# An MLP's down projection as seven block products in place of eight, woven with the up projection

## The chip, the core and the metric

The kernel runs on one core of a Trainium2 chip. The core has a matrix engine (TensorE, PE in the rows), a vector engine (VectorE, DVE), a scalar engine (ScalarE, ACT), GpSimd (POOL) and SyncE (SP), which here only issues transfers. PE reads its operands from the on-chip memory SBUF and writes sums to PSUM, which has eight banks of 128 partitions by 512 fp32 numbers. The metric is the device time of one execution in microseconds (us), lower is better.

## What is computed

One decoder layer in fp32 on 512 tokens of 2048 columns:

```
u  = rms_norm(x, norm1_w)
P  = u @ w_in                       # conv groups and gated delta heads work on P
h1 = x + concat(conv_out, delta_out) @ w_out
m  = rms_norm(h1, norm2_w) @ w_mlp_up           # 2048 x 8192
h2 = h1 + square(relu(m)) @ w_mlp_down          # 8192 x 2048
y  = rms_norm(h2, final_norm_w)
```

The change concerns the last product and what stands around it. Everything up to the output projection (`w_out`) is computed as before.

## The kernel before

**Products.** Every fp32 matrix product is made of three fp32r matmuls: each operand is split in an upper part (fp32r) and the rest, and `mm3` (lines 153 to 156 in the rows) adds upper x upper, upper x rest and rest x upper in PSUM. One matmul has a 128x128 stationary and a 128x512 moving operand. `load_pair` (L145 the load on SP, L149 ACT's cast to the upper part `whi`, L150 DVE's subtraction for the lower part `wlo`) brings a weight tile of 256 x 512 (512 KB) in a ring of three raw buffers and four pairs of split ones.

**The mixers** (conv groups and delta heads) take the first 700 us. Their buffers come from the pools `row_pool`, `inv_pool` and `tmp`, which stay open to the end of the kernel.

**Output projection.** For each of four column stretches `dc` of 512, eight weight tiles go through PE into four banks `po`, one for each 128 tokens. Then x is loaded again into `h1` and added (L739), and the squares are summed for the second norm. `norm2_columns` transposes h1 into `u2T`, 16 pairs of tiles of 128 columns by 512 tokens, without the row factors.

**The MLP** goes through 16 blocks `fb` of 512 hidden columns. `up_block(fb)` has eight steps `u`; each loads one weight tile and issues 24 matmuls into four banks `pu` (hidden columns by tokens). Then for each bank ACT takes the relu (L778), DVE multiplies it with the bank (L780), ACT and DVE split the square (L782, L783) into `hh` and `hl`, which lie in buffers of the mixers. `down_block(fb)` has eight weight tiles, two for each column stretch `dc`; each issues 24 matmuls (hidden tile stationary, weights moving) into four banks `pd`. After the second tile of a `dc` DVE adds the four banks to h1 with the squared row factor `r2`, one fp32 number for each token (L802). Since relu(r u)^2 = r^2 relu(u)^2 for r > 0, the row factors wait until there.

```
    hid = up_block(0)
    for fb in range(1, NFB):
        nxt = up_block(fb)
        down_block(fb - 1, hid)
        hid = nxt
```

So 192 matmuls of up are followed by 192 of down, 15 times; the last down product (`pl`, L833 to L842) has its 16 weight tiles split ahead of time into the buffers that `u2T` leaves, goes by tokens, and ends in the final norm (L841 to L854).

**What sets the order.** A scheduler places the instructions of each engine by the data they need and the priorities in the code (`tc.high_priority`); buffers of a pool are handed out in the order in which they come free. Weight loads are pulled ahead as far as their rings allow. PSUM: four banks in `ps_mm` (`po`, `pu`), four in `ps_aux` (`pd`, `pl`, small things).

Of the kernel before, what the change touches and what calls it, by code (L numbers as in the profile page):

```python
# [45 lines left out]
def tile_hybrid_block(ctx: ExitStack, tc: tile.TileContext, x, norm1_w, w_in, b_glu, dw_w, dw_b,  # L46
# [10 lines left out]
    row_pool = ctx.enter_context(tc.tile_pool(name="rowp", bufs=1))  # L57
# [42 lines left out]
    upper = const.tile([P, P], F32, name="upper")  # L100
# [5 lines left out]
    strict_r = const.tile([P, P], F32R, name="strict_r")  # L106
# [9 lines left out]
    sc_cols = const.tile([P, WSHORT, 3 * NH], F32, name="sc_cols")  # L116
    dw_cols = const.tile([P, WCONV, NG], F32, name="dw_cols")
# [35 lines left out]
    def mm3(ps, sta, mov, start, stop):  # L153
        nc.tensor.matmul(ps, lhsT=sta[0], rhs=mov[0], start=start, stop=False)  # L154
        nc.tensor.matmul(ps, lhsT=sta[0], rhs=mov[1], start=False, stop=False)  # L155
        nc.tensor.matmul(ps, lhsT=sta[1], rhs=mov[0], start=False, stop=stop)  # L156
# [50 lines left out]
    def transpose_half(i, groups):  # L207
        """Tokens 256 i to 256 i + 255; groups of pairs of column tiles, with their banks."""
# [110 lines left out]
    def decay_columns(pabT):  # L319
# [6 lines left out]
        ab = small.tile([P, NT, 16], F32, tag="ab", bufs=1, name="ab")  # L326
# [3 lines left out]
        def st(name, shape=(P, NT, NH)):  # L330
            return small.tile(list(shape), F32, tag=name, bufs=1, name=name)
# [28 lines left out]
        gh = small.tile([P, 2, NT, NH], F32R, tag="gh", bufs=1, name="gh")  # L360
# [72 lines left out]
    def head_keys(h, pk):  # L433
        # decay[s, c] = exp(sum of g over s < t <= c), c >= s
# [39 lines left out]
    def invert_blocks(bt, keys):  # L474
        """Transposed inverses of the 32-row diagonal blocks of I - na, by substitution."""
# [37 lines left out]
        # the transposes of y's left blocks: columns 0..63 for the blocks of 32, 64..127 for 64  # L513
# [41 lines left out]
        # upper blocks of 32, then of 64: y12 = y11 na12 y22, both blocks of a size in 64 columns  # L555
# [157 lines left out]
    for dc in range(4):  # L713
        ds = slice(dc * 512, (dc + 1) * 512)
        ps = [ps_mm.tile([P, SEQ], F32, tag="mm", name=f"po{dc}{t}") for t in range(NT)]
        for r in range(NH):
# [17 lines left out]
            if dc == 3 and 1 <= r <= 6:  # L734
                norm2_columns(range(2 * r - 2, 2 * r))
        for t in range(NT):
            h1[t][dc] = row(f"h1_{t}{dc}")
            nc.sync.dma_start(h1[t][dc], x[t * P:(t + 1) * P, ds])
            nc.vector.tensor_add(h1[t][dc], ps[t], h1[t][dc])  # L739
            square_sum(h1[t][dc], ss2[t][:, dc:dc + 1], f"j2{t}{dc}", nc.scalar)  # L740
# [14 lines left out]
    HID_TAGS = ("ug", "q", "v", "kg", "kd", "vr", "it", "y", "xx", "pc", "c0", "c1", "c2", "c3")  # L755

    def hid_pair(fb, j):
        i = (fb % 2) * 4 + j
        if i < 7:
            return (tt(HID_TAGS[2 * i], f"hh{fb}_{j}", (P, SEQ), F32R),  # L760
                    tt(HID_TAGS[2 * i + 1], f"hl{fb}_{j}", (P, SEQ), F32R))
        return tuple(row_pool.tile([P, SEQ], F32R, tag=f"row{r}", name=f"hr{fb}_{j}_{r}")
                     for r in free_rows[:2])

    def up_block(fb):
# [19 lines left out]
        return hid

    def down_block(fb, hid):
        for dc in range(4):
            ds = slice(dc * 512, (dc + 1) * 512)
            ps = [ps_aux.tile([P, SEQ], F32, tag="aux", name=f"pd{fb}_{dc}{t}") for t in range(NT)]  # L790
            for u in range(2):
                r0 = fb * FB + u * 256
                w = load_pair(w_down[r0:r0 + 256, ds].rearrange("(k p) c -> p k c", p=P),
                              [P, 2, 512], f"d{fb}_{dc}{u}")
                for t in range(NT):
                    cs = slice(t * P, (t + 1) * P)
                    for i in range(2):
                        m = hid[2 * u + i]
                        mm3(ps[t], (m[0][:, cs], m[1][:, cs]), (w[0][:, i], w[1][:, i]),
                            start=(u == 0 and i == 0), stop=(u == 1 and i == 1))  # L800
# [80 lines left out]
```

## Time and profile before

| | |
|---|---|
| three runs | 2291.12, 2291.35 and 2291.99 us, median 2291.35 |
| span of the profiled execution, first to last instruction | 2290.3 us |
| median of the runs less that span | 1.05 us |
| PE busy in the span | 2239.9 us (98%) |
| DVE, ACT, GpSimd busy | 1172.6, 691.1, 222.5 us |
| MLP | from 888.5 us to the end |

The page has the busy time of each engine over the whole span, then the span in 40 slices, the transfers, the chain of work that ended last, and groups of instructions by source line with mean durations. A matmul's row shows 389 ns, but matmuls overlap; their pace is read from how many start in a stretch. PEld is the load of a stationary operand, which goes beside PE. PEclk is the granted share of PE's full clock: 1.00 is 2.4 GHz, 0.50 is 1.2 GHz. "[4.38 <-PE pu L155]" behind a row of the timeline is the idle time of that engine before the row and the instruction that ended it.

### The profile page before, as it was taken

To read this page: it belongs to the slowest core of one execution; us is meant where nothing else is said; L and a number is where in the kernel's file an instruction comes from. 1 tells how busy PE (TensorE), PEld (TensorE's weight loads), DVE (VectorE), ACT (ScalarE), POOL (GpSimd) and SP (SyncE) were. 2 spreads that over 40 slices of the span, in tenths; PEclk is the share of its full clock that TensorE was granted. 3 is DMA by queue.
4 is the path that set the end of the run, shared out by engine and by line. 5 is a ranking of instruction groups with operands and counts; after the bars stand their busy time and mean duration, and the time that the engine had idled before them with its cause. 6 is when DMAs were issued, how large, how long until landed. Compare 5 with 4: busy or idle time off the path is not lost.

```text
span 2290.3 us, 25927 instructions
## 1 busy us (share of the span) xinstructions
PE 2239.9 (98%) x10431; PEld 1857.1 (81%) x10431; DVE 1172.6 (51%) x1671; ACT 691.1 (30%) x1153; POOL 222.5 (10%) x261
## 2 busy tenths in 40 slices
PE   6989999989999999999999999999999999999998
PEld 5877888868888888888888888888888888888886
DVE  6578677678776334344354353353353343343355
ACT  5333443324344223222122122222122222122132
POOL 3481110471110000000000000000000000000000
PEclk9999999989999999999999999999999999999999
DMA  5323223232324333333333333333333333333342
GB/s 163 106 71 83 78 79 97 79 79 77 85 83 140 100 92 92 92 101 92 101 94 100 93 101 94 99 95 98 98 96 99 95 100 93 102 92 101 92 137 84
DMA packets 189766, 220.67 MB, mean 96 GB/s; under 512 B 9901, under 2 KB 108622, under 8 KB 189646
## 3 DMA queue, kind: packets, MB, share of 16 engines
q1 hardware_dynamic: 188238, 215.34, 32.3%
q0 software_dynamic: 1408, 3.67, 0.5%
q8 instruction: 82, 1.34, 0.2%
q14 instruction: 38, 0.31, 0.0%
HBM read 212.17 MB, written 6.82 MB: 96 GB/s over the span
## 4 chain that ended last, share of the span: by engine, by line
PE 88%; POOL 6%; DVE 2%; issue 2%; DMA 2%; ACT 0%; SPq 0%; POOLq 0%; DVEq 0%; ACTq 0%
PE pu L155 10%; PE pu L154 10%; PE pu L156 10%; PE pd L154 10%; PE pd L156 10%; PE pd L155 10%; PE po L156 3%; PE po L154 3%; PE po L155 3%; POOL inv_g L496 2%; POOL inv_t L494 2%; PE pin_k L154 1%; PE pin_k L155 1%; PE pin_g L154 1%; PE pin_z L154 1%
## 5 line engine op out<-in xcount | busy, mean ns | idle before, releaser
L154 PE MATMUL pu<-v_h,whi_u 128*128 128x512 f32 x1024 | 398.4, 389 | 0.0
L155 PE MATMUL pu<-v_l,whi_u 128*128 128x512 f32 x1024 | 398.3, 389 | 0.0
L156 PE MATMUL pu<-v_h,wlo_u 128*128 128x512 f32 x1024 | 398.3, 389 | 0.0
L150 DVE TENSOR_TENSOR wlo_u<-wraw_u,whi_u 128x1024 fp32r<-128x1024 f32 x128 | 156.8, 1225 | 413.6 <-ACT whi_u L149 413.6
L154 PE MATMUL pd<-whi_d,hh 128*128 128x512 f32 x848 | 329.9, 389 | 0.0
L155 PE MATMUL pd<-wlo_d,hh 128*128 128x512 f32 x848 | 329.9, 389 | 0.0
L156 PE MATMUL pd<-whi_d,hl 128*128 128x512 f32 x848 | 329.9, 389 | 0.0
L149 ACT CAST whi_u<-wraw_u 128x1024 fp32r<-128x1024 f32 x128 | 135.0, 1055 | 543.2 <-PE pu L155 285.8
L150 DVE TENSOR_TENSOR wlo_d<-wraw_d,whi_d 128x1024 fp32r<-128x1024 f32 x120 | 147.0, 1225 | 295.6 <-ACT whi_d L149 295.6
L149 ACT CAST whi_d<-wraw_d 128x1024 fp32r<-128x1024 f32 x120 | 126.6, 1055 | 417.0 <-PE pd L156 216.0
L154 PEld LDWEIGHTS pu<-v_h,whi_u 128*128 128x128 f32 x1024 | 192.2, 188 | 39.9
L156 PEld LDWEIGHTS pu<-v_h,wlo_u 128*128 128x128 f32 x1024 | 192.2, 188 | 39.9
L155 PEld LDWEIGHTS pu<-v_l,whi_u 128*128 128x128 f32 x1024 | 192.2, 188 | 39.8
L802 DVE SCALAR_TENSOR_TENSOR h<-pd,r,h 128x512 f32<-128x512 f32 x240 | 174.4, 747 | 62.4 <-PE pd L156 62.4
L381 DVE SCALAR_TENSOR_TENSOR cacc<-chh,dw_cols,cacc 128x511 f32<-128x511 f32 (+14 forms) x240 | 195.5, 815 | 8.4 <-ACT cacc L378 5.1
L154 PEld LDWEIGHTS pd<-whi_d,hh 128*128 128x128 f32 x848 | 159.2, 188 | 33.1
L155 PEld LDWEIGHTS pd<-wlo_d,hh 128*128 128x128 f32 x848 | 159.2, 188 | 33.0
L156 PEld LDWEIGHTS pd<-whi_d,hl 128*128 128x128 f32 x848 | 159.2, 188 | 33.1
L167 POOL TENSOR_TENSOR rs_rf<-rs_sf,neg_half 128x1 f32<-128x1 f32 x4 | 2.2, 546 | 1549.0 <-DVE rs_sf L165 1549.0
L154 PE MATMUL po<-whi_o,m_h 128*128 128x512 f32 x256 | 101.0, 394 | 0.0
L156 PE MATMUL po<-whi_o,m_l 128*128 128x512 f32 x256 | 100.2, 391 | 0.0
L155 PE MATMUL po<-wlo_o,m_h 128*128 128x512 f32 x256 | 99.9, 390 | 0.0
(291 smaller groups left out, 3400.1 us busy)
## 6 DMA issues: line engine op xcount, KB each, us to landing
wraw_u<-in_w_mlp_up SPq DMA_DIRECT2D x128, 512.0 KB, 3.7
wraw_d<-in_w_mlp_down SPq DMA_DIRECT2D x120, 512.0 KB, 3.6
wraw_o<-in_w_out SPq DMA_DIRECT2D x32, 512.0 KB, 4.2
wraw_k<-in_w_in SPq DMA_DIRECT2D x16, 512.0 KB, 4.1
wraw_a<-in_w_in SPq DMA_DIRECT2D x16, 512.0 KB, 3.7
wraw_g<-in_w_in SPq DMA_DIRECT2D x16, 512.0 KB, 3.8
wraw_q<-in_w_in SPq DMA_DIRECT2D x16, 512.0 KB, 3.7
wraw_v<-in_w_in SPq DMA_DIRECT2D x16, 512.0 KB, 3.8
```

Source lines behind the costliest of these rows:

```text
L149: nc.scalar.copy(hi, raw)
L150: sub.tensor_sub(lo, raw, hi.bitcast(F32))
L154: nc.tensor.matmul(ps, lhsT=sta[0], rhs=mov[0], start=start, stop=False)
L155: nc.tensor.matmul(ps, lhsT=sta[0], rhs=mov[1], start=False, stop=False)
L156: nc.tensor.matmul(ps, lhsT=sta[1], rhs=mov[0], start=False, stop=stop)
L167: nc.gpsimd.tensor_tensor(rr, s, neg_half[:, 0:1], ALU.pow)
L381: nc.vector.scalar_tensor_tensor(acc[:, j:], hh[:, :SEQ - j], dw_cols[:, WCONV - 1 - j, g:g + 1], acc[:, j:], ALU.mult, ALU.add)
L494: nc.gpsimd.tensor_mul(tv, a[:, j:j + 1, j + 1:].to_broadcast([n, j + 1, w]), g[:, :j + 1, j:j + 1].to_broadcast([n, j + 1, w]))
L496: nc.gpsimd.tensor_add(g[:, :j + 1, j + 1:], g[:, :j + 1, j + 1:], tv)
L802: nc.vector.scalar_tensor_tensor(h1[t][dc], ps[t], r2[t], h1[t][dc], ALU.mult, ALU.add)
```

## The change

**Seven products.** In blocks 0 to 14 the down product of a block is taken as a 2 x 2 product of blocks: tokens in halves of 256, hidden columns in halves of 256, output columns in two halves, done twice (`c` = 0, 1) for 512 columns of each half. `down_block(fb, left)` makes seven products by Strassen's scheme (in Winograd's form) in place of eight: the weight tiles wd11, wd21, wd12, wd22 are loaded raw (pool `mlp`, tag `wd`, five buffers), four sums of 128x1024 (`sub`, L842) are made of them, and each of the seven left and right factors is split. A product is 12 matmuls into a pair of banks, `px` or `py` (pool `ps_pair`, two pairs). Some products go on accumulating in a pair that has already been added to h1 once: the pair is read after the first product and again after the next one that accumulates on it, so one partial sum serves two quarters of the output. There are seven adds of 128x1024 to h1 (L854) for each `c`.

**Left factors.** The row factor r is spread along the free dimension once (`r_rows`: `rstd_rows`, a diagonal, one fp32 matmul with ones into `pr`, a copy), and applied ahead of the square: `m1` = max(pu, 0) * r_rows on DVE (L793), squared by ACT into quarters `a` (tokens by hidden columns). `split_sums` makes four sums (L810 to L816) and seven splits of 128x512 (casts on ACT; L803 on DVE). The adds to h1 no longer have a factor.

**Weave.** The steps of the up block of `fb` and the products of `fb - 1` alternate: up0, up1, two products, up2, two products, and so on to up7, two products.

**Buffers.** Mixer constants that lay in `const` and `small` move to pools that close with the mixers (`mixers.close()` behind the first column stretch of the output projection); the new pools `h1p` and `mlp` lie over their memory. h1 is now kept as tiles of two token tiles (128 x 2 x 512). `ps_aux` closes before the MLP and `ps_pair` takes its banks; `pl` moves to `ps_mm`. The last block's hidden tiles are made by `take_last`.

The diff, cut to its core:

```diff
+        if dc == 0:
+            mixers.close()
+            h1_pool = ctx.enter_context(tc.tile_pool(name="h1p", bufs=1, reuse_waits="tile"))
+            mlp = ctx.enter_context(tc.tile_pool(name="mlp", bufs=1, reuse_waits="tile"))
...
+    r_diag = mlp.tile([P, NT, P], F32, tag="m1", bufs=2, name="r_diag")
     for t in range(NT):
-        s = small.tile([P, 1], F32, tag="rs_s", name=f"r2{t}")
...
+        rr = rstd_rows(small, ss2[t], 1.0 / D, f"m{t}")
+        nc.vector.tensor_scalar(r_diag[:, t], ident, rr, None, ALU.mult)
+    pr = ps_aux.tile([P, SEQ], F32, tag="aux", name="pr")
+    nc.tensor.matmul(pr, lhsT=ones, rhs=fl(r_diag), start=True, stop=True)
+    r_rows = mlp.tile([P, SEQ], F32, tag="r_rows", name="r_rows")
+    nc.scalar.copy(r_rows, pr)
+    aux_banks.close()
+    ps_pair = ctx.enter_context(tc.tile_pool(name="ps_pair", bufs=2, space=PSUM, reuse_waits="tile"))
...
+                        m1 = mlp.tile([P, SEQ], F32, tag="m1", bufs=2, name=f"m1{fb}_{j}")
+                        nc.vector.scalar_tensor_tensor(m1, ps[j], 0.0, r_rows, ALU.max, ALU.mult)
+                        out(j, m1)
...
+        a11, a12, a21, a22 = (a[:, i] for i in range(4))
+        s1 = mlp.tile([P, 2, 256], F32, tag="s1", name=f"s1_{fb}")
+        with tc.high_priority(offset=4000):
+            p0, p1 = split(a11, 0), split(a12, 1)
+            nc.vector.tensor_add(s1, a21, a22)
+            p5 = split(s1, 3)
+            nc.vector.tensor_sub(s1, s1, a11)
+            p6 = split(s1, 2)
+            nc.vector.tensor_sub(a21, a11, a21)
+            p7 = split(a21, 4)
+            nc.vector.tensor_sub(a12, a12, s1)
+            p3 = split(a12, 5)
+            p4 = split(a22, 6)
...
+            def product(i, ps, w, first):
+                for t in range(2):
                     cs = slice(t * P, (t + 1) * P)
...
+                    for k in range(2):
+                        mm3(ps[:, t], (left[i][0][:, k, cs], left[i][1][:, k, cs]),
+                            (w[0][:, k], w[1][:, k]), start=(first and k == 0), stop=(k == 1), more=not first)
...
+            b11, b21 = raw(0, 0, "wd11"), raw(1, 0, "wd21")
+            w = split(b11, 0)
+            px = pair("px")
+            product(0, px, w, True)
+            add(0, 0, px)
+            b22, b12 = raw(1, 1, "wd22"), raw(0, 1, "wd12")
+            yield
+            w = split(b21, 1)
+            pz = pair("py")
+            product(1, pz, w, True)
+            add(0, 0, pz)
+            sub(b11, b12, b11)
+            t2 = mlp.tile([P, 2, 512], F32, tag="wd", bufs=DRAW, name=f"wdt_{fb}{c}")
+            sub(t2, b22, b11)
+            yield
+            w = split(t2, 2)
+            product(2, px, w, False)
+            add(0, 1, px)
+            sub(b21, b21, t2)
...
+        for u in range(KT // 2):
+            next(up)
+            if u > 0:
+                next(down, None)
+                next(down, None)
```

The change in the order on PE. Before, where one column stretch of block 4 ends and the next begins (`pd4_13` is its fourth bank, `d4_11` and `d4_20` weight tiles, `hh`, `hl` the split hidden tiles):

```order
L154 MATMUL pd4_13_10269<-whi_d4_11_10302,hh4_3_9646 128x512
L155 MATMUL pd4_13_10269<-wlo_d4_11_10303,hh4_3_9646 128x512
L156 MATMUL pd4_13_10269<-whi_d4_11_10302,hl4_3_9647 128x512
L154 MATMUL pd4_20_10334<-whi_d4_20_10340,hh4_0_9622 128x512
L155 MATMUL pd4_20_10334<-wlo_d4_20_10341,hh4_0_9622 128x512
```

A bank of its own is filled over two weight tiles, 24 matmuls each, and four other banks follow. Now, where the seventh product of the first half (`px40`, factor `sh4_6`) ends and the first of the second half (`px41`, factor `sh4_0`) begins:

```order
L160 MATMUL px40_10091<-whi_d406_10290,sh4_6_10014 128x512
L161 MATMUL px40_10091<-wlo_d406_10291,sh4_6_10014 128x512
L162 MATMUL px40_10091<-whi_d406_10290,sl4_6_10015 128x512
L160 MATMUL px41_10315<-whi_d410_10311,sh4_0_9986 128x512
L161 MATMUL px41_10315<-wlo_d410_10312,sh4_0_9986 128x512
```

A product has a weight tile and 12 matmuls of its own, and the next half's first pair follows directly; an up step stands before and after these two products.

The change on DVE at the border of two blocks. Before (block 4's down product begins: `wlo_d4` are its weight splits, `m25`, `hl5`, `hr5` the hidden tiles of block 5):

```order
L150 TENSOR_TENSOR wlo_d4_11_10303<-wraw_d4_11_10300,whi_d4_11_10302 128x1024
L783 TENSOR_TENSOR hl5_2_10187<-m25_2_10184,hh5_2_10186 128x512
L780 SCALAR_TENSOR_TENSOR m25_3_10192<-pu5_3_9925,rl5_3_10190 128x512
L783 TENSOR_TENSOR hr5_3_16_10195<-m25_3_10192,hr5_3_12_10194 128x512
L150 TENSOR_TENSOR wlo_d4_20_10341<-wraw_d4_20_10338,whi_d4_20_10340 128x1024
L802 SCALAR_TENSOR_TENSOR h1_00_6482<-pd4_00_10198,r20_7438,h1_00_6482 128x512
L802 SCALAR_TENSOR_TENSOR h1_10_6487<-pd4_01_10199,r21_7442,h1_10_6487 128x512
L802 SCALAR_TENSOR_TENSOR h1_20_6492<-pd4_02_10200,r22_7446,h1_20_6492 128x512
L802 SCALAR_TENSOR_TENSOR h1_30_6497<-pd4_03_10201,r23_7450,h1_30_6497 128x512
```

Splits of weights, four hidden tiles and one group of four 128x512 adds stand loosely beside each other. Now, behind block 5's up matmuls (`sl5` are the lower left factors, `s1` and `a5` sums and quarters, `px41`, `py41` the last two products of block 4, `wlo_d500` the split for the first product of block 5):

```order
L854 TENSOR_TENSOR h1_03_7389<-py41_10367,h1_03_7389 128x1024
L803 TENSOR_TENSOR sl5_1_10553<-a5_10018,sh5_1_10552 128x512
L803 TENSOR_TENSOR sl5_3_10558<-s1_5_10547,sh5_3_10557 128x512
L814 TENSOR_TENSOR a5_10018<-a5_10018 128x512
L854 TENSOR_TENSOR h1_11_6758<-px41_10315,h1_11_6758 128x1024
L812 TENSOR_TENSOR s1_5_10547<-s1_5_10547,a5_10018 128x512
L803 TENSOR_TENSOR sl5_4_10568<-a5_10018,sh5_4_10567 128x512
L816 TENSOR_TENSOR a5_10018<-a5_10018,s1_5_10547 128x512
L803 TENSOR_TENSOR sl5_2_10563<-s1_5_10547,sh5_2_10562 128x512
L803 TENSOR_TENSOR sl5_6_10577<-a5_10018,sh5_6_10576 128x512
L803 TENSOR_TENSOR sl5_5_10573<-a5_10018,sh5_5_10572 128x512
L837 TENSOR_TENSOR wlo_d500_10650<-wd11_50_10645,whi_d500_10649 128x1024
```

Nine of the eleven instructions on the left factors, two of the adds and the split that the first product of the next block reads now stand in a row; nine more stand directly ahead of these (the add before those two, the splits of two up tiles, four `m1`, one left split and one left sum), 21 in all.

## Rows read from the trace of the kernel before

**Rows 1.** The page: span, and busy us of each engine (share of the span).

```profile
span 2290.3 us, 25927 instructions
PE 2239.9 (98%) x10431; PEld 1857.1 (81%) x10431; DVE 1172.6 (51%) x1671; ACT 691.1 (30%) x1153; POOL 222.5 (10%) x261
```

**Rows 2.** Table by stretches of 200 us; busy us and instructions of each engine.

```profile
core 0: us, PE busy (x) PEld busy (x) DVE busy (x) ACT busy (x) POOL busy (x), PEclk, DMA share, GB/s
...
200.00:400.00 200.00, 199.90 (x1037) 166.28 (x1036) 150.91 (x258) 78.52 (x185) 28.20 (x27) 1.00 0.31 85
...
1000.00:1200.00 200.00, 200.00 (x884) 165.62 (x883) 82.69 (x94) 47.95 (x53) 0.00 (x0) 1.00 0.33 98
```

**Rows 3.** The page: chain that ended last, by engine and by line.

```profile
PE 88%; POOL 6%; DVE 2%; issue 2%; DMA 2%; ACT 0%; SPq 0%; POOLq 0%; DVEq 0%; ACTq 0%
PE pu L155 10%; PE pu L154 10%; PE pu L156 10%; PE pd L154 10%; PE pd L156 10%; PE pd L155 10%; PE po L156 3%; PE po L154 3%; PE po L155 3%; POOL inv_g L496 2%; POOL inv_t L494 2%; PE pin_k L154 1%; PE pin_k L155 1%; PE pin_g L154 1%; PE pin_z L154 1%
```

**Rows 4.** Groups by line and shape, 900 to 2250 us: busy us, mean ns | idle before.

```profile
L154 PE MATMUL pd<-whi_d,hh 128*128 128x512 f32 x848 | 329.9, 389 | 0.0
...
L802 DVE SCALAR_TENSOR_TENSOR h<-pd,r,h 128x512 f32<-128x512 f32 x240 | 174.4, 747 | 62.4 <-PE pd L156 62.4
...
L150 DVE TENSOR_TENSOR wlo_d<-wraw_d,whi_d 128x1024 fp32r<-128x1024 f32 x120 | 147.0, 1225 | 295.6 <-ACT whi_d L149 295.6
...
L149 ACT CAST whi_d<-wraw_d 128x1024 fp32r<-128x1024 f32 x120 | 126.6, 1055 | 417.0 <-PE pd L156 216.0 <-PE pu L155 197.3 <-issue 3.4
```

**Rows 5.** Timeline of the MLP: one weight tile; start us, us, instruction.

```profile
1203.94 0.39 PE L156 MATMUL pu<-v_h,wlo_u 128*128 128x512 f32 x1
...
1204.14 1.05 ACT L149 CAST whi_u<-wraw_u 128x1024 fp32r<-128x1024 f32 x1 [4.38 <-PE pu L155]
...
1205.23 1.23 DVE L150 TENSOR_TENSOR wlo_u<-wraw_u,whi_u 128x1024 fp32r<-128x1024 f32 x1 [4.21 <-ACT whi_u L149]
```

**Rows 6.** Groups by line and shape, same stretch as in rows 4.

```profile
L780 DVE SCALAR_TENSOR_TENSOR m<-pu,rl 128x512 f32<-128x512 f32 x64 | 43.9, 685 | 10.7 <-ACT rl L778 10.7
...
L783 DVE TENSOR_TENSOR hl<-m,hh 128x512 fp32r<-128x512 f32 x56 | 38.5, 687 | 6.9 <-ACT hh L782 5.5
L778 ACT ACTIVATE rl<-pu 128x512 f32<-128x512 f32 x64 | 38.1, 595 | 20.7 <-PE pu L156 20.7
L782 ACT CAST hh<-m 128x512 fp32r<-128x512 f32 x56 | 34.6, 618 | 15.9 <-DVE m L780 15.9
```

**Rows 7.** The adds of the output projection: ns min/median/max, first and last start us.

```profile
L739 DVE TENSOR_TENSOR h<-po,h x16: 678/688/692, 748.0 to 887.1; 128x512 f32<-128x512 f32 x16
```

**Rows 8.** Table of the transfers: issues, KB each, median us from issue to landing.

```profile
wraw_d<-in_w_mlp_down SPq DMA_DIRECT2D x120, 512.0 KB, 3.6
...
h<-in_x SPq DMA_DIRECT2D x16, 256.0 KB, 3.5
```

**Rows 9.** Timeline of DVE: a 128x1024 split, and the instruction behind it.

```profile
2200.98 1.23 DVE L150 TENSOR_TENSOR wlo_d<-wraw_d,whi_d 128x1024 fp32r<-128x1024 f32 x1 [1.86 <-ACT whi_d L149]
2202.12 1.40 DVE L802 SCALAR_TENSOR_TENSOR h<-pd,r,h 128x512 f32<-128x512 f32 x2
```

**Rows 10.** Timeline of PE where the output projection ends.

```profile
886.89 1.91 PE L202 MATMUL pt_v<-ident,h 128*128 128x128 f32 x16
888.55 0.48 PE L154 MATMUL pu<-v_h,whi_u 128*128 128x512 f32 x1
```

**Rows 11.** Timeline of SP at the end of the first column stretch.

```profile
748.06 5.84 SPq L145 DMA_DIRECT2D wraw_o<-in_w_out  x2
```

**Rows 12.** Timeline of PE: instructions behind its longer idles.

```profile
22.91 0.29 PE L316 MATMUL pabT<-u_l,ab_w 128*16 128x256 f32 x1 [1.95 <-DVE rs_sx L164]
...
155.21 1.12 PE L539 MATMUL ptv<-ident,v 128*128 128x128 f32 x4 [5.22 <-DVE v L425]
...
173.87 0.90 PE L389 MATMUL cpt<-ident,cacc 128*128 128x128 f32 x3 [5.28 <-DVE cacc L381]
...
488.98 0.90 PE L539 MATMUL ptv<-ident,v 128*128 128x128 f32 x3 [5.22 <-DVE v L425]
...
507.62 0.90 PE L389 MATMUL cpt<-ident,cacc 128*128 128x128 f32 x3 [4.93 <-DVE cacc L381]
```

**Rows 13.** Table of the 5 us from those instructions on; columns as in rows 2.

```profile
22.90:27.90 5.00, 4.53 (x36) 4.05 (x37) 4.73 (x15) 3.91 (x9) 2.94 (x3) 1.00 0.87 262
155.20:160.20 5.00, 4.99 (x20) 4.42 (x21) 4.89 (x6) 4.34 (x19) 4.61 (x6) 0.71 0.27 80
173.90:178.90 5.00, 5.00 (x15) 4.09 (x16) 3.54 (x11) 0.00 (x0) 1.37 (x2) 0.53 0.19 42
489.00:494.00 5.00, 5.00 (x19) 4.38 (x20) 4.89 (x6) 4.31 (x19) 4.61 (x6) 0.63 0.26 79
507.70:512.70 5.00, 5.00 (x14) 4.13 (x15) 3.59 (x11) 0.00 (x0) 1.32 (x2) 0.50 0.19 43
```

More of the change, by code (lines that the diff above doesn't have):

```diff
@@ L29 @@
 EPS = 1e-6
+DRAW = 5
 NPK, TAPS, Y_PTK, Y_PX2 = 2, 3, 6, 1
@@ L99, in tile_hybrid_block @@
     nc.gpsimd.memset(ones, 1.0)
-    upper = const.tile([P, P], F32, name="upper")
+    upper = mixc.tile([P, P], F32, name="upper")
     nc.gpsimd.affine_select(out=upper, in_=ones, compare_op=ALU.is_ge, fill=0.0, base=0,
@@ L151, in load_pair, with mm3 @@
         return hi, lo
[L153 to L156, printed above, removed]
+    def mm3(ps, sta, mov, start, stop, more=False):
+        nc.tensor.matmul(ps, lhsT=sta[0], rhs=mov[0], start=start, stop=False, skip_group_check=more)
+        nc.tensor.matmul(ps, lhsT=sta[0], rhs=mov[1], start=False, stop=False, skip_group_check=more)
+        nc.tensor.matmul(ps, lhsT=sta[1], rhs=mov[0], start=False, stop=stop, skip_group_check=more)
     def act_pair(name):
@@ L325, in decay_columns @@
                                 ident[:32, :32])
-        ab = small.tile([P, NT, 16], F32, tag="ab", bufs=1, name="ab")
+        ab = mixc.tile([P, NT, 16], F32, tag="ab", bufs=1, name="ab")
         nc.vector.tensor_copy(ab, pab[:, :, 0])
@@ L330, in st @@
         def st(name, shape=(P, NT, NH)):
-            return small.tile(list(shape), F32, tag=name, bufs=1, name=name)
+            return mixc.tile(list(shape), F32, tag=name, bufs=1, name=name)
         beta = st("beta")
@@ L785, in up_block @@
[L785 to L795, printed above, removed]
-                    cs = slice(t * P, (t + 1) * P)
[L797 to L800, printed above, removed]
-            for t in range(NT):
-                nc.vector.scalar_tensor_tensor(h1[t][dc], ps[t], r2[t], h1[t][dc], ALU.mult, ALU.add)
@@ new lines, in up_block, with split_sums, split @@
+            yield
+    def split_sums(a, fb):
+        def split(src, i):
+            hi = mlp.tile([P, 2, 256], F32R, tag=f"sh{i}", name=f"sh{fb}_{i}")
+            lo = mlp.tile([P, 2, 256], F32R, tag=f"sl{i}", name=f"sl{fb}_{i}")
+            nc.scalar.copy(hi, src)
+            nc.vector.tensor_sub(lo, src, hi.bitcast(F32))
+            return hi, lo
+        a11, a12, a21, a22 = (a[:, i] for i in range(4))
+        s1 = mlp.tile([P, 2, 256], F32, tag="s1", name=f"s1_{fb}")
+        with tc.high_priority(offset=4000):
+            p0, p1 = split(a11, 0), split(a12, 1)
[8 more added lines that the diff above has]
+            p4 = split(a22, 6)
+        return p0, p1, p6, p5, p7, p3, p4
@@ new lines, in take_quarters, with out, take_last @@
+    def take_quarters(a):
+        def out(j, m1):
+            for th in range(2):
+                nc.scalar.activation(a[:, 2 * th + j // 2, j % 2], m1[:, th * 256:(th + 1) * 256], AF.Square)
+        return out
+    last = []
+    def take_last(j, m1):
+        m2 = mlp.tile([P, SEQ], F32, tag="m1", bufs=2, name=f"m2_{j}")
+        nc.scalar.activation(m2, m1, AF.Square)
+        hi = mlp.tile([P, SEQ], F32R, tag=f"sh{j}", name=f"hh{j}")
+        lo = mlp.tile([P, SEQ], F32R, tag=f"sl{j}", name=f"hl{j}")
+        nc.scalar.copy(hi, m2)
+        nc.vector.tensor_sub(lo, m2, hi.bitcast(F32))
+        last.append((hi, lo))
@@ new lines, in tile_hybrid_block @@
+    left = None
+    for fb in range(NFB):
+        if fb < NFB - 1:
+            a = mlp.tile([P, 4, 2, 256], F32, tag="quarters", name=f"a{fb}")
+            up = up_block(fb, take_quarters(a))
+        else:
+            up = up_block(fb, take_last)
+        down = down_block(fb - 1, left) if fb else iter(())
+        for u in range(KT // 2):
[3 more added lines that the diff above has]
+                next(down, None)
+        for _ in up:
+            pass
+        if fb < NFB - 1:
+            left = split_sums(a, fb)
+        for _ in down:
+            pass
@@ L835, in tile_hybrid_block @@
         for dc in range(4):
-            ps = ps_aux.tile([P, SEQ], F32, tag="aux", name=f"pl{t}{dc}")
+            ps = ps_mm.tile([P, SEQ], F32, tag="mm", name=f"pl{t}{dc}")
             for k in range(4):
-                mm3(ps, (hid[k][0][:, cs], hid[k][1][:, cs]), last_w[4 * dc + k],
+                mm3(ps, (last[k][0][:, cs], last[k][1][:, cs]), last_w[4 * dc + k],
                     start=(k == 0), stop=(k == 3))
-            h = h1[t][dc]
-            nc.vector.scalar_tensor_tensor(h, ps, r2[t], h, ALU.mult, ALU.add)
-            square_sum(h, ss3[t][:, dc:dc + 1], f"j3{t}{dc}", nc.scalar, "z")
+            h = h1_row(t, dc)
+            nc.vector.tensor_add(h, ps, h)
+            junk = mlp.tile([P, SEQ], F32, tag="m1", bufs=2, name=f"j3{t}{dc}")
+            nc.scalar.activation(junk, h, AF.Square, accum_out=ss3[t][:, dc:dc + 1])
             if dc < 3:
```

119 lines of the change are left out of this document (72 added, 47 removed).

## The prediction

> **What bounds the kernel now.** I read the page's engine line first: TensorE (PE) is busy for 2239.9 us of a span of 2290.3 us, the vector engine (DVE) for 1172.6, the scalar engine (ACT) for 691.1 [rows 1]. A share over the whole span hides stages, so the table by stretches came next. From 1000 to 1200 us, which is MLP like all of 900 to 2250, PE is busy in 200.00 of 200 us at a granted clock of 1.00 (2.4 GHz) with 884 matmuls, DVE in 82.69, ACT in 47.95, and the DMA engines a third of the time [rows 2]. So the MLP is paced by nothing but the number of matmuls, one every 200 / 884 = 0.2262 us. The chain that ended last says the same: PE has 88% of it, and the lines of `mm3` for `pu` and `pd` lead it [rows 3]. Then I looked for what lies close behind PE. The time that L802 shows idle is DVE waiting for PE [rows 4]. The timeline of one weight tile shows ACT's cast released by PE when an old tile came free, and the lower half ready 2.3 us later at 1206.46 [rows 5]. With four tiles in the ring, each of 24 matmuls or 5.43 us, three tiles (16.3 us) lie between the release and the use, so it is ready 14 us early. Nothing but PE sets the time here, and DVE has more than half of its own time free.
>
> **What the change removes.** Of each of 15 down blocks it takes 24 matmuls: 14 products of 12 instead of 8 weight tiles of 24, so 168 for 192. Shapes stay 128x128 by 128x512, with the same three forms. 15 x 24 = 360, and 360 x 0.2262 = **81.4 us**, all on the path as long as PE never waits. A block (360 matmuls in place of 384) then lasts 81.4 us instead of 86.9.
>
> **What it adds beside PE.** Per block DVE now has 22 splits and 8 weight sums of 128x1024 at 1.225 us (L150's row [rows 4]; the sums have the same shape), 14 adds of 128x1024 from PSUM, and 15 instructions of 128x512 (4 `m1`, 4 left sums, 7 left splits) at 0.69 us [rows 6]. The PSUM adds have no row of their size. From below, a 128x512 add (0.688) and the 0.538 by which the SBUF rows grow from 512 to 1024 give 1.226; from above, two 128x512 adds, 2 x 0.688, give 1.38 [rows 7]; the 128x512 forms from PSUM and from SBUF are 688 and 687 ns [rows 6, 7], so I take 1.225. The sum is 44 x 1.225 + 15 x 0.69 = 64.2 us of 81.4, or 79% (66.4 at the upper price). ACT has 22 x 1.055 + 7 x 0.618 + 8 squares of 128x256, which lie between half of and a whole `rl` of 0.595 (I take 0.40): 30.7 us, 38%. Both fit on the average. SP issues 16 loads of 512 KB per block as before, each landing 3.6 us after issue [rows 8]; the same bytes in 81.4 us raise 98 GB/s to 105.
>
> **Where it could wait: the block boundary.** I walked the order of the changed kernel with these durations and 0.2 us per handover. Let up7 start at S. PE then takes up7 (5.43), two products (5.43), up0 and up1 (10.86), and reaches the next block's first product P0 at S + 21.7. Ahead of P0's lower split DVE has, in its own order, 3 PSUM adds, the splits of up0, up1 and of P0 itself, 4 `m1` and 11 left-operand instructions: 6 x 1.225 + 15 x 0.69 = 17.7 us. The first add can start at S + 0.2, the `m1` wait for up7's end, and the last add waits for the second product, at S + 10.9. With these waits P0's split ends at S + 19.3. That leaves **2.4 us**, the smallest margin that I find. P1's split is done at 20.5 for 24.4, P2's split and P0's add at 29.1 for 32.6, P3's at 31.6 for 35.3. The bounds of the walk: at 1.38 per PSUM add it ends 0.5 later; the timeline starts a vector instruction 1.14 us after one of 1.23 [rows 9], and at that pitch six wide ones end 0.5 earlier. Neither uses the margin up. The Trainium skill, "VectorE: DVE Perf Modes", section "The DRAIN you can't avoid", says that the next instruction starts only when the pipe has emptied; 1.14 after 1.23 shows starts that overlap a little. By the page the walk stands as it is, by the row it is 0.5 us better; the sum is the same by either.
>
> **Mid-block.** P0' (first product of the second half) takes the PSUM pair that came free first, that of P5, since the pools hand pairs out by release; the built order's wait there is for P5's add, which ends while PE is still in the products ahead. With T the end of up4, P1' takes the pair of P6, whose add ends by T + 4.7, against T + 10.9. Raw buffers: each load waits for the split that read the buffer five loads ago, also early. So I cost the weave at 0; its cover is the up tiles between the products, 5.43 us each, without which a split, an add and 4/7 of a weight sum per product (2.57 x 1.225 = 3.1 us) would exceed the 2.71 of 12 matmuls.
>
> **What it adds on the path.** (a) The row factors: one fp32 matmul of 128x512. No row has it; 16 fp32 transposes of 128 columns take 888.55 - 886.89 = 1.66 us [rows 10], so 512 columns cost 4 / 16 of that, 0.4, from the nearest row, from below one ordinary pitch, 0.23; twice the nearest row, 0.9, from above. I take 0.6. Its chain (sums, power, diagonal) runs beside the 5.43 us of up0's matmuls. (b) h1's loads move behind the last weights of the first output column, because the pools of the mixers must close first. The first add of that column runs at 748.0 now [rows 7], and SP is busy with weights from 748.06 [rows 11]; with 3.5 us from issue to landing [rows 8] they come at some 752 to 753, while PE has one bank's matmuls (2.7 us) and then needs the next bank emptied. I take +1, from 0 to 4 (one landing). (c) The end: `take_last` starts only 5.4 us before the final products, where before a whole down block of 43 us lay between. Four instructions of about 0.65 us in a chain, four hidden tiles deep, take some 6 us: +0.7, from 0 to 3. The final row adds cost 0.688 for 0.75, not on a chain that moves. Sum: +2.3.
>
> **Forecast.** 2290.3 of span and 1.05 around it make the median of 2291.35. 2291.35 - 81.4 + 2.3 = **2212 us**, with its own bounds 2206 to 2222 (addends at 0.2 and at 8, and 4 us, 0.3% of the MLP, for the pitch).
>
> **Rivals.** (1) *DVE late at the boundary.* If casts and splits of the left operands alternate without overlap, each of the 7 splits waits a cast of 0.618 and two handovers of 0.2, which adds up to 7 us to the 19.3; in the trace before, the like of it cost only 6.9 us over 56 `hl` splits [rows 6], 0.12 each. In between, 1 to 3 us over the margin cost 15 each: 2227 to 2257. (2) *The same place, slower than before*: the saving is used up when each boundary idles (81.4 - 2.3) / 15 = 5.3 us, so when P0's split is 7.7 us later than walked. Idles of 4.93 to 5.28 us also drop the clock: the 5 us after them run at 0.50 to 0.71, while after 1.95 us it stayed at 1.00 [rows 12, 13]; mean loss (0.29 + 0.47 + 0.37 + 0.50) / 4 x 5 = 2.04 us. With that the turn is already at 3.2 to 5.3 us of idle. At 9 us late: 15 x (6.6 + 2.04) = 130, so 2342; at 8 us without the clock 2296. For it speaks that DVE has these 21 instructions in a row there with three waits on ACT and PE; against it that every one of them would have to be 0.37 us longer than its row. (3) *Pairs used in turn*: if P0' waited for P6's add at T + 4.9 instead of starting at T + 2.7, 2.2 us x 15 = 33: 2245. The built wait says otherwise. The Trainium skill, "TensorE: Matmul & The Clock Gate", section "A second HAM failure mode: psum-queue depth-cycling", has a rule against cycling PSUM banks each iteration: the small idles between groups make the clock fall and rise. No stretch of the MLP shows such an idle here [rows 2], and 1.95 us kept the clock; as a mechanism of this kernel it would add 15 x 2.04 = 31 to this rival: 2276. (4) *Contention or pace*: DVE at 79% and PE read the same memory. In the stretch 200 to 400 us DVE is busy for 150.91 of 200 and PE still for 199.90 at 1.00 [rows 2]; one per cent of 1350 us would give 2226, and the whole saving is gone only at 6%. (5) *It does not save*: the weave would have to leave PE idle by what it removes, 2285 to 2295; the built order holds the 360 matmuls fewer.
>
> **How the numbers follow.** Forecast 0.68; (1) 0.12; (2) 0.06; (3) 0.04 with the clock's case in it; (4) 0.06; (5) 0.04. Two in ten may be left out: I leave out (2), (5), the upper part of (1) and of (3), and keep the rest, 2205 to 2242. A difference of 0.2% (4.6 us) is about what a measurement of this kernel can tell from none. Faster: 0.68 + 0.12 + 0.04 + 0.06 + half of (5) = 0.92; slower 0.06; same 0.02.
>
> **What would show it.** In the changed profile: PE busy for 200 of 200 us in the MLP with 884 matmuls still, DVE near 158 and ACT near 75 per 200 us, at clock 1.00; no idle of PE ahead of P0 with DVE's lower split as its releaser; a block every 81.4 us. An idle there of d us per block makes the time 2212 + 15 d. DVE adds of clearly over 1.38 us, or a first-product idle ahead of `px` of the second half, would prove the walk wrong, and matmuls fewer than 884 per 200 us at clock 1.00 the pace.

## The result and the profile after

The changed kernel takes 2234.41 us (median of 4 runs, 2233.93 to 2235.85), the kernel before 2291.23 in the same comparison: ratio 0.9754, 95% interval 0.974 to 0.9768, so 57 us or 2.5% faster. The profiled execution has a span of 2232.5 us, 57.8 less than the 2290.3 of [rows 1]. That is inside the range (2205 to 2242) and on the forecast side, but 22 us above the forecast of 2212: the change brought 57 of the 79 us expected.

The page of the changed kernel, engine line and chain, as in [rows 1, 3]:

```profile
PE 2180.1 (98%) x10073; PEld 1791.1 (80%) x10073; DVE 1542.3 (69%) x1956; ACT 815.1 (37%) x1349; POOL 224.2 (10%) x265
...
PE 88%; POOL 6%; DVE 2%; DMA 2%; issue 1%; ACT 0%; SPq 0%; POOLq 0%; DVEq 0%; ACTq 0%
PE pu L162 10%; PE pu L161 10%; PE pu L160 10%; PE px L161 5%; PE px L160 5%; PE px L162 5%; PE py L161 4%; PE py L160 4%; PE py L162 4%; PE po L160 3%; PE po L162 3%; PE po L161 2%; POOL inv_g L502 2%; POOL inv_t L500 2%; PE pin_k L160 1%
```

The table by stretches of 200 us (columns as in [rows 2]), and the groups from 900 to 2200 us that answer to [rows 4, 6]:

```profile
1000.00:1200.00 200.00, 200.00 (x872) 163.38 (x871) 149.77 (x151) 74.24 (x98) 0.00 (x0) 1.00 0.34 100
...
1400.00:1600.00 200.00, 200.00 (x872) 163.22 (x871) 144.66 (x142) 72.80 (x95) 0.00 (x0) 1.00 0.35 105
```

```profile
L161 PE MATMUL pu<-v_l,whi_u 128*128 128x512 f32 x1017 | 395.6, 389 | 0.0
...
L160 PE MATMUL px<-whi_d,sh 128*128 128x512 f32 x480 | 189.6, 395 | 0.0
...
L854 DVE TENSOR_TENSOR h<-px,h 128x1024 f32<-128x1024 f32 x120 | 146.7, 1222 | 33.4 <-PE px L162 33.4
...
L842 DVE TENSOR_TENSOR wd<-wd,wd 128x1024 f32<-128x1024 f32 x60 | 73.2, 1221 | 0.5
...
L803 DVE TENSOR_TENSOR sl<-a,sh 128x512 fp32r<-128x512 f32 x75 | 50.4, 687 | 0.7
...
L900 ACT ACTIVATE a<-m 128x256 f32<-128x256 f32 x120 | 41.9, 407 | 30.4 <-DVE m L793 30.0
```

PE is still busy for 200.00 of 200 us at clock 1.00, and the chain is PE's: no new wait took the place of an old one. DVE (149.77 and 144.66 us) and ACT (74.24 and 72.80) stay below what the walk gave (158 and 75). But PE starts 872 matmuls in 200 us where it started 884. By the prediction's own test that is the pace, not a wait. The first two of the groups show where: a product's matmul lasts 395 ns, an up matmul 389 as before. The timeline of PE at the end of a product and the start of an up step (start us, duration us):

```profile
1201.70 0.39 PE L160 MATMUL py<-whi_d,sh 128*128 128x512 f32 x1
1201.93 0.40 PE L161 MATMUL py<-wlo_d,sh 128*128 128x512 f32 x1
1202.17 0.39 PE L162 MATMUL py<-whi_d,sl 128*128 128x512 f32 x1
1202.40 0.40 PE L160 MATMUL py<-whi_d,sh 128*128 128x512 f32 x1
...
1203.09 0.39 PE L160 MATMUL pu<-v_h,whi_u 128*128 128x512 f32 x1
1203.32 0.39 PE L161 MATMUL pu<-v_l,whi_u 128*128 128x512 f32 x1
1203.55 0.39 PE L162 MATMUL pu<-v_h,wlo_u 128*128 128x512 f32 x1
1203.77 0.39 PE L160 MATMUL pu<-v_h,whi_u 128*128 128x512 f32 x1
```

Three product matmuls take 1202.40 - 1201.70 = 0.70 us, three up matmuls 1203.77 - 1203.09 = 0.68. Taken over all starts of the trace, products come every 233.3 ns and up matmuls every 226.7; in the trace before `pu` and `pd` both came every 226.7. It is the same in every block: from one block's P0 to the next takes 82.72 us, 14 times, and 192 x 0.2267 + 168 x 0.2333 = 82.7. With 226.7 for both it would be 81.6.

The ledger of the spans, from the first and last starts of `po`, `pu` and `pl` matmuls in both traces:

| stretch | before, us | after, us | difference |
|---|---|---|---|
| start to the last `po` matmul | 886.66 | 891.28 | +4.62 |
| to the first `pl` matmul | 1351.11 | 1287.98 | -63.13 |
| to the last `pl` matmul | 43.29 | 44.56 | +1.27 |
| to the end | 9.23 | 8.70 | -0.53 |

The second line is -81.6 for the 360 matmuls, +16.8 for 2520 product matmuls 6.67 ns slower, +1.6 for the fp32 matmul of the row factors, and 0.1 of rest. The third line is the same 6.67 ns on the 192 `pl` matmuls. So 18.1 of the 22 us missing are pace.

### The profile page after: what moved, and what is told of

Its sections match the earlier page's. It is cut to its first block, busy times and chain, and to the rows that moved or that the text cites. A ratio compares the mean times of both kernels' runs of the same rounds, so it can differ in the third digit from the quotient of the medians.

```text
span 2232.5 us, 25987 instructions
## 1 busy us (share of the span) xinstructions
PE 2180.1 (98%) x10073; PEld 1791.1 (80%) x10073; DVE 1542.3 (69%) x1956; ACT 815.1 (37%) x1349; POOL 224.2 (10%) x265
## 4 chain that ended last, share of the span: by engine, by line
PE 88%; POOL 6%; DVE 2%; DMA 2%; issue 1%; ACT 0%; SPq 0%; POOLq 0%; DVEq 0%; ACTq 0%
PE pu L162 10%; PE pu L161 10%; PE pu L160 10%; PE px L161 5%; PE px L160 5%; PE px L162 5%; PE py L161 4%; PE py L160 4%; PE py L162 4%; PE po L160 3%; PE po L162 3%; PE po L161 2%; POOL inv_g L502 2%; POOL inv_t L500 2%; PE pin_k L160 1%
## 5 line engine op out<-in xcount | busy, mean ns | idle before, releaser
L837 DVE TENSOR_TENSOR wlo_d<-wd,whi_d 128x1024 fp32r<-128x1024 f32 x180 | 218.5, 1221 | 253.3 <-ACT whi_d L836 253.3
L836 ACT CAST whi_d<-wd 128x1024 fp32r<-128x1024 f32 x180 | 188.7, 1048 | 464.6 <-PE pu L161 285.4
L160 PE MATMUL px<-whi_d,sh 128*128 128x512 f32 x480 | 189.6, 395 | 0.0
L161 PE MATMUL px<-wlo_d,sh 128*128 128x512 f32 x480 | 189.6, 395 | 0.0
L162 PE MATMUL px<-whi_d,sl 128*128 128x512 f32 x480 | 189.2, 394 | 0.0
L854 DVE TENSOR_TENSOR h<-px,h 128x1024 f32<-128x1024 f32 x120 | 146.7, 1222 | 33.4 <-PE px L162 33.4
L160 PE MATMUL py<-whi_d,sh 128*128 128x512 f32 x360 | 142.2, 395 | 0.0
L161 PE MATMUL py<-wlo_d,sh 128*128 128x512 f32 x360 | 142.2, 395 | 0.0
L162 PE MATMUL py<-whi_d,sl 128*128 128x512 f32 x360 | 141.9, 394 | 0.0
L854 DVE TENSOR_TENSOR h<-py,h 128x1024 f32<-128x1024 f32 x90 | 110.0, 1222 | 27.4 <-PE py L162 26.3
```

The lines of the kernel that those rows point to most:

```text
L836: nc.scalar.copy(hi, src)
L837: nc.vector.tensor_sub(lo, src, hi.bitcast(F32))
L854: nc.vector.tensor_add(h, ps, h)
```

## Experiments: why the products are slower

Everything that a row of the trace names was the same as before: shapes, types, three forms, clock. The built program shows what no row does, the addresses. In the changed kernel the constants lost tiles to the mixers' pool, and 32 bytes of offset came about: every buffer of `act_pool` and `w_pool` begins 32 bytes past a multiple of 64 in its partition, while the left factors in the new pool `mlp` (and the last block's `hh`, `hl`) begin at a multiple of 64. So an up matmul has both operands at 32, a product one at 32 and one at 0. Before, all were at 0. Theory: a matmul whose two operands begin at different places modulo 64 bytes costs 6.67 ns more. (64 is the theory's period; in the built programs the two starts differ by a multiple of 256 bytes, or by 32 bytes beside one, so the runs cannot tell it from 128 or 256.) Rivals: the pairs of PSUM banks; PE and a busier DVE sharing memory.

**e1** moves the MLP's pool by 32 bytes:

```diff
             mlp = ctx.enter_context(tc.tile_pool(name="mlp", bufs=1, reuse_waits="tile"))
+            mlp.tile([P, 8], F32, tag="pad_m", name="pad_m")
```

> In the changed kernel the product matmuls start every 233.3 ns, the up matmuls every 226.7. By the built program, both operands of the up matmuls begin 32 bytes past a multiple of 64 in their partition; in the products the moving weights do, the left factors do not. This kernel is the changed one with 32 bytes of padding at the start of the MLP's pool, so that the left factors begin at 32 as well; no instruction is added. Theory (operand start addresses): product pitch falls to 226.7, 15 x 168 + 192 matmuls x 6.67 ns = 18.1 us less: 2216. Rival 1 (PSUM pairs, or vector engine and PE sharing memory): pitch stays 233.3, time 2234. Rival 2 (a moving operand off 64 costs by itself, and the up matmuls hide it): pitch stays 233.3.

**e2** moves every operand of the MLP's matmuls to a multiple of 64: e1's line, and ahead of the first constant

```diff
+    const.tile([P, 8], F32, name="pad_c")
     ident = const.tile([P, P], F32, name="ident")
```

> The changed kernel with 32 bytes of padding ahead of the constants and 32 at the start of the MLP's pool: every matmul operand of the MLP begins at a multiple of 64 bytes, as in the kernel before. Theory: product pitch 226.7, time 2216, and if the first 700 us lost their 2.7 us to addresses too, 2213. Rival 1 (PSUM pairs or shared memory): 233.3 ns and 2234 us.

**e3** has the second line alone, so that the weights come to 0 and the left factors, which move along, to 32.

> The changed kernel with 32 bytes of padding ahead of the constants alone: in the products the moving weights now begin at a multiple of 64, the left factors 32 past one, the reverse of the changed kernel. If it is the difference of the two operands that costs, 233.3 ns and 2234 us; if it is the moving operand alone, 226.7 and 2216; with PSUM pairs or shared memory as the cause, 233.3 and 2234 too, so this run tells the form of the rule apart, not the cause.

**e4** makes the same mismatch in the kernel before: the padding of the constants, and one in the pool behind the weights:

```diff
+    small.tile([P, 8], F32, tag="pad_s", bufs=1, name="pad_s")
```

> The kernel before with two paddings of 32 bytes, which put its weights 32 past a multiple of 64 and leave the hidden tiles hh and hl at a multiple of 64: no Strassen, no pairs, no extra vector work. Theory (operand start addresses): pd and pl pitch 233.3 in the 2544 + 144 matmuls with these tiles, x 6.67 ns = 17.9 us, time 2309. Rival 1 (PSUM pairs or shared memory): 226.7 ns and 2291 us.

Measured, with the start-to-start pitch of all product (or `pd`) matmuls in each trace (e1 and e2 have four runs each, spread over 4.7 and 3.6 us; e3 to e11 are single runs):

| run | moving, stationary (modulo 64) | pitch, ns | time, us |
|---|---|---|---|
| before | 0, 0 | 226.7 | 2291.2 |
| changed | 32, 0 | 233.3 | 2234.4 |
| e1 | 32, 32 | 226.7 | 2216.4 (ratio 0.9665, 0.9651 to 0.968) |
| e2 | 0, 0 | 226.7 | 2217.2 (ratio 0.9672, 0.9655 to 0.9688) |
| e3 | 0, 32 | 233.3 | 2234.8 |
| e4 (kernel before) | 32, 0 | 232.8 | 2313.1 |

The stretches of e1 and e4 (columns as in [rows 2]; first e1, then e4):

```profile
1000.00:1200.00 200.00, 200.00 (x884) 165.65 (x883) 151.74 (x153) 75.53 (x99) 0.00 (x0) 1.00 0.34 101
```

```profile
1000.00:1200.00 200.00, 200.00 (x871) 163.19 (x870) 83.25 (x93) 47.66 (x53) 0.00 (x0) 1.00 0.32 95
```

884 matmuls again in e1, with DVE as busy as in the changed kernel and the same pairs of banks; 871 in e4, without pairs, with DVE at 83 us and nothing woven. That excludes both rivals. e3 excludes the moving operand alone, and e1 shows that 32 as such costs nothing: what costs is the difference of the two. e4's pitch is a mean over 2544 matmuls of this kind and 336 with `hr` tiles, which lie at 32 like the weights. Its trace has both kinds side by side: from one matmul with `hh` or `hl` to the next 233.3 ns (2424 steps), from one with `hr` to the next 227.5 (224 steps). e4's time, 2313.1, stands 20 us above the 2292.9 of the kernel before in the same comparison, for 17.9 of the theory; 2 of the 20 lie ahead of the last `po` matmul. Eight words of padding give 18 us: **e1 and e2 beat both kernels**, by 3.3% against the kernel before. What was not tried: offsets other than 32 bytes, other types, other widths. Why the engine takes longer is not shown.

What cost the 2.7 us in the first 700 us stays open. In the traces of the kernels made from the changed one the first `po` matmul starts between 695.8 and 698.9 us (697.6 in the changed kernel itself, 694.9 in the kernel before, 696.9 in e4), so single traces differ by as much, and no run was made for it.

## Experiments: the margin, the pairs and the weave

These start from e2, so that the pace is out of the way.

**e5, pairs in turn.** The first product of the second half (P0') has to take `px` and wait for P6's add:

```diff
-                return ps_pair.tile([P, 2, SEQ], F32, tag="pair", name=f"{name}{fb}{c}")
+                return ps_pair.tile([P, 2, SEQ], F32, tag=name, bufs=1, name=f"{name}{fb}{c}")
```

> e2_all_64 with a pool tag of its own for each of the two PSUM pairs, one buffer each, so that the first product of the second half (P0') has to take px and wait for the add of P6, which ends px's use; nothing else changes in what is computed. The add starts 0.36 us after PE and takes 1.23, with 0.2 of handover: 1.8 us of PE idle at each of 15 places, +27: 2244. If idles of this size also drop the clock (as those of 4.93 us did), +2.04 each: 2275. If P0' did not get the other pair in the changed kernel at all (the prediction's reading of the order wrong), no change: 2217.

**e6, e7, a late split.** DVE makes the lower split for each block's first product 4 times (e6) or 8 times (e7):

```diff
-                    nc.vector.tensor_sub(lo, src, hi.bitcast(F32))
+                    for _ in range(4 if c == i == 0 else 1):
+                        nc.vector.tensor_sub(lo, src, hi.bitcast(F32))
```

> e2_all_64 in which DVE makes the lower split of each block's first product 4 times in place of once (the same values), 3 more 128x1024 instructions at the pitch of 1.14 us. The built order puts the splits of the second product and of up2 between them, so the last copy ends 5 x 1.14 = 5.7 us later than now. The trace of e2 has this split ready 4.35 us ahead of its product, and the second matmul is the first to need it (+0.23). Theory (a margin of 4.6 us, smallest at this place): idle of 1.1 to 1.3 us at 15 places, +17 to +20: 2234 to 2237. If something else hides the delay: 2217.

> The same with 8 copies, 7 more: the last ends 9 x 1.14 = 10.3 us later. Theory: idle of 5.7 to 5.9 us at 15 places, +86 to +89: 2303 to 2306; if such idles also drop the clock (2.04 us each), 2334 to 2337. The slope between this run and the one with 3 should be 15 us for each us of delay, without the clock.

All three missed: 2219.1 us (e5, expected 2244), 2216.8 (e6, 2234 to 2237) and 2232.6 (e7, 2303 to 2306). In e5 and e6 PE stays busy for 200.00 of 200 us. The built order explains it: the scheduler plans PE's order too, saw the longer wait, and pulled other matmuls ahead. In e5 nine matmuls of up5 now stand before P0', in e6 six of the second product stand between the first and second matmul of the first, in e7 a whole product and 16 matmuls of up2. Only in e7 is there too little to pull ahead; two short waits a block are left, which with the slower starts behind them make 1.07 us, 15 in 14 blocks (engine and line, what it waited for: us in total, times, longest us):

```profile
PE px L161 <- DVE h L857: 4.0, 14, 0.3
PE pu L161 <- ACT whi_u L155: 2.8, 14, 0.2
```

So these runs tell nothing of the margin, but they do tell that a wait which the scheduler foresees is mostly filled. To measure the margin, the order must be held. **e9** is e5, **e10** is e6 and **e11** is e7 with each matmul of the MLP kept in program order, which is the order of e2 but for `pr`, the matmul of the row factors: in e2 it stands among block 0's up matmuls, here ahead of them:

```diff
+            if in_mlp:
+                tc.keep_in_program_order(ins)
```

> In the run with pairs in turn the scheduler had moved 9 matmuls of up5 ahead of the first product of the second half, and PE never idled. Here the MLP's matmuls are kept in the order of the code, which is the order of e2_all_64, so that this product stands directly behind P6 and waits for P6's add. Theory: idle of 1.8 us at 15 places, 2217 + 27 = 2244; with the clock dropping behind such idles, 2275. If the wait costs nothing even so: 2217.

> The kernel with 4 copies of the lower split of each block's first product, with the MLP's matmuls kept in the order of e2_all_64 (in the run before the scheduler had put six matmuls of the second product ahead). The last copy ends 5 x 1.14 = 5.7 us later than in e2, where the margin was 4.35 + 0.23 us. Theory: idle of 1.1 to 1.3 us at 15 places, 2217 + 17 to 20 = 2234 to 2237.

> The same with 8 copies: the last ends 9 x 1.14 = 10.3 us later. Theory: idle of 5.7 to 5.9 us at 15 places, 2303 to 2306 without a drop of the clock; 2334 to 2337 with 2.04 us each for the clock, as behind the idles of 4.93 to 5.28 us in the trace before.

2277.3 us (e9), 2245.8 (e10), 2350.8 (e11). The waits of PE from `pr` on, of e9, of e10 and of e11:

```profile
PE px L163 <- DVE h L859: 29.7, 15, 2.5
...
PE pr L770 <- DVE r_diag L768: 5.1, 1, 5.1
```

```profile
PE px L163 <- DVE wlo_d L843: 15.6, 14, 1.1
...
PE pr L770 <- DVE r_diag L768: 5.1, 1, 5.1
```

```profile
PE px L163 <- DVE wlo_d L843: 91.0, 15, 6.2
...
PE pr L770 <- DVE r_diag L768: 5.1, 1, 5.1
```

The margin at the block's border follows from two runs: in the traces the split ends 5.8 us later than in e2 and PE idles 1.1 us (4.7), or 10.8 later and 6.2 (4.6). In the changed kernel itself P0's split ends 4.50 us ahead of P0 in 14 of the 15 blocks, and 14 us ahead in the first. Two rows of its timeline (DVE's and PE's) show one: DVE makes the splits of P0 and P1 from 1191.78 on, 1.22 us for the first, so to 1193.00, and PE starts P0 at 1197.50:

```profile
1191.78 2.35 DVE L837 TENSOR_TENSOR wlo_d<-wd,whi_d 128x1024 fp32r<-128x1024 f32 x2
...
1197.50 0.39 PE L160 MATMUL px<-whi_d,sh 128*128 128x512 f32 x1
```

The span of e10's trace is 30.3 us above e2's: 14 idles of 1.1 with a short catch-up behind each (1.44 us a time, 20.1 together), some 6 for the one-time wait of `pr`, and 2.8 ahead of the MLP. e9 and e11 have the wait of `pr` too, and cost more than it and their idles, 60 us for 29.7 and 134 for 91.0. The timeline of PE in e9 shows why, at P0' (idle before it and releaser in brackets):

```profile
1159.34 0.39 PE L163 MATMUL px<-whi_d,sl 128*128 128x512 f32 x1
1161.67 0.54 PE L163 MATMUL px<-whi_d,sh 128*128 128x512 f32 x1 [1.94 <-DVE h L859]
1162.01 0.63 PE L163 MATMUL px<-wlo_d,sh 128*128 128x512 f32 x1
1162.43 0.63 PE L163 MATMUL px<-whi_d,sl 128*128 128x512 f32 x1
...
1165.39 0.40 PE L163 MATMUL px<-whi_d,sh 128*128 128x512 f32 x1
1165.62 0.40 PE L163 MATMUL px<-wlo_d,sh 128*128 128x512 f32 x1
```

```profile
1161.67:1165.17 3.50, 3.50 (x9) 2.75 (x10) 0.98 (x1) 0.00 (x0) 0.00 (x0) 0.54 0.34 96
1165.62:1169.12 3.50, 3.50 (x17) 2.87 (x16) 2.36 (x2) 1.05 (x1) 0.00 (x0) 1.00 0.06 19
```

After 1.94 us of idle nine matmuls come some 0.43 us apart, at a granted clock of 0.54, near the level of 1.2 GHz; then 1.00 again. That is 1.7 us on top of the idle. It happens behind 13 of e9's 15 idles. Behind the other two, of the same 1.94 us, the clock stays at 1.00; one of them:

```profile
1417.96 0.47 PE L163 MATMUL px<-whi_d,sh 128*128 128x512 f32 x1 [1.94 <-DVE h L859]
1418.27 0.40 PE L163 MATMUL px<-wlo_d,sh 128*128 128x512 f32 x1
1418.50 0.39 PE L163 MATMUL px<-whi_d,sl 128*128 128x512 f32 x1
```

```profile
1417.96:1421.46 3.50, 3.50 (x16) 2.90 (x17) 1.48 (x2) 0.45 (x1) 0.00 (x0) 1.00 0.32 92
```

So e9's 60 us are 15 idles that each delay PE by 2.1 (32), 13 x 1.7 of clock (22) and some 6 for `pr`. In [rows 12, 13] too an idle of 1.95 us kept the clock at 1.00: the length of an idle alone does not tell, and what decides is not shown. e10's 1.1 us kept it behind every idle (1.00 from 1000 to 2200 us). In e11 the clock costs 1.5 to 3.0 us behind an idle of 6.2 (4.9 in the first block), 2.3 in the mean. The Trainium skill, "TensorE: Matmul & The Clock Gate", section "A second HAM failure mode: psum-queue depth-cycling", tells of a bf16 kernel that cycles through PSUM banks, where brief idles of PE between the groups send the clock back and forth between its two levels; e9's trace agrees in 13 of its 15 idles. The changed kernel cycles through the same pairs without an idle, and the clock stays at 1.00.

**e8, no weave.** All eight up steps of a block, then the 14 products of the block before in one stretch (the left sums move behind them):

```diff
             next(up)
-            if u > 0:
-                next(down, None)
-                next(down, None)
```

> e2_all_64 without the weave: all eight up tiles of a block, then the 14 products of the block before in one stretch. A product of 12 matmuls lasts 2.72 us, and for each DVE has a split, an add and 4/7 of a weight sum: 2.57 x 1.14 = 2.9 us, and a product must wait for the add of the one before the last on its pair. Theory: at least 14 x 0.2 = 3 us of idle per block, +45: 2262; with the waits for adds (0.5 to 1 us at 12 products) up to +180: 2400. Rival (the weave buys nothing, the splits run ahead in the ring): 2217.

2270.5 us, 53 above e2 and within the expected span. The waits of PE and one stretch (columns as in [rows 2]):

```profile
PE px L161 <- ACT whi_d L838: 20.0, 14, 1.4
PE py L161 <- ACT whi_d L838: 6.2, 14, 0.4
PE px L162 <- DVE wlo_d L839: 1.8, 10, 0.2
```

```profile
1000.00:1200.00 200.00, 194.03 (x827) 157.82 (x826) 148.36 (x146) 70.63 (x89) 0.00 (x0) 0.97 0.31 97
```

The waits sum up to 28 us, and the clock falls to 0.97 here (0.98 or 0.99 in the stretches from 1200 to 2200 us); the weave is worth these 53 us, two thirds of what the missing matmuls bring.

## Why the prediction held in part, point by point

- **The bound and the removed matmuls: right.** PE is the bound before and after, and 360 matmuls at their pace are 81.6 us of the second line of the ledger.
- **"Shapes stay the same": the step that failed.** The sum took 0.2262 us for every matmul because shape and form were those of rows that it had. The pace also hangs on where the operands begin, and the pools had moved; term mis-sized: 2712 matmuls by 6.67 ns, 18.1 us. It was rival (4), "pace", with 6 in 100 and 14 us; its mechanism as written, DVE and PE sharing memory, is refuted by e1. That 2234 lies in the range is in part luck: the pace alone had been put at 2226, and what the range holds above that was kept for idles at the border and ahead of P0', which did not come.
- **Nothing waits at the border or mid-block: right.** P0's margin is the smallest, as walked, at 4.5 us for 2.4. The walk was too careful: the `m1` of the first banks start before up7 ends, and DVE's starts overlap. The PSUM add of 128x1024 takes 1222 ns, the lower bound chosen.
- **P0' gets the pair of P5: right.** With the pair of P6 and the order held (e9) the idles cost 32 us and the clock 22, for the 33 + 31 of rival (3). The one row with 1.95 us, held against the clock's part, was no guide: 13 of e9's 15 idles lowered it.
- **"An idle of d us makes 2212 + 15 d": right only for a given order** (e10; in e11 with the clock's share on top). That a late split would be seen as an idle at all was wrong: e5 to e7 show the scheduler filling it. So rival (2) would have needed a delay that the scheduler did not foresee.
- **(a) The row factors**: 1.6 us for 0.6. The matmul is two instructions, together 1.10 us, and waits 0.51 for `r_diag`; the two steps from the up matmul ahead of it to the second one behind it take 2.06 us, where two ordinary ones take 0.45. **(b) h1's loads**: PE waits 0.21 and 0.93 us for the first adds, in all 1.9 for 1. **(c) The end**: 0.5 faster where 0.7 slower was taken. Together they come to 3.0 for the 2.3 of the sum; the 2.7 us ahead of the MLP were in no term.

The rows of (a) and (b) in the changed kernel:

```profile
754.12 0.50 PE L160 MATMUL po<-whi_o,m_h 128*128 128x512 f32 x1 [0.21 <-DVE h L754]
...
757.39 0.50 PE L160 MATMUL po<-whi_o,m_h 128*128 128x512 f32 x1 [0.93 <-DVE h L754]
```

```profile
897.59 0.39 PE L161 MATMUL pu<-v_l,whi_u 128*128 128x512 f32 x1
898.49 1.10 PE L766 MATMUL pr<-r_diag,ones 128*128 128x512 f32 x2 [0.51 <-DVE r_diag L764]
899.02 0.79 PE L162 MATMUL pu<-v_h,wlo_u 128*128 128x512 f32 x1
899.65 0.39 PE L160 MATMUL pu<-v_h,whi_u 128*128 128x512 f32 x1
```

## What to carry to other kernels

A duration from a row holds for an operation of the same shape only if its operands lie alike: when an edit moves pools, compare the start addresses of both matmul operands, and pad one by 32 bytes where they differ by 32 bytes beside a multiple of 64 (differences of 64 or 128 bytes were not tried). Where a scheduler orders the engines, a wait that you add in the code need not appear as a wait; read the new order before costing it, and hold the order when you want to measure a margin. A product scheme that trades matmuls for vector work pays most when that work is woven into stretches where PE has other matmuls: here it brings 74 us with the weave and 21 without.

## What the runs showed of the hardware beyond that

- fp32r matmuls of 128x128 by 128x512 start every 226.7 ns when both operands begin at the same place modulo 64 bytes (0 and 0, or 32 and 32; the starts then differed by a multiple of 256 bytes), and every 233.3 when one begins at 32 and the other at 0, in either order.
- Idles of 1.94 us (one of 2.5) in a stretch where PE otherwise ran without a pause were followed by matmuls at the lower clock level, 1.7 us a time, in 13 of 15 cases; two of 1.94 us, and one of 1.95 us near the start of the kernel before, were not.
- A vector instruction of 128x1024 that reads two PSUM banks takes 1222 ns, as one from SBUF (1221).
